# Products with the low halves of the weights, emitted two parts of the stream later

## The chip, the cores and the metric

The kernel runs on one core of one Trainium2 chip. The time is that of one execution on the device, in microseconds (us). Before the change it is 3813.72 us, the median of three runs (3813.32 to 3816.19).

## The reference

Two transformer blocks in float32 follow each other, for 256 tokens and 2048 features. The first mixes with an mLSTM and an S5 recurrence and has PEER (products with 16384 experts) in place of an FFN. The second is modulated by a vector `c` through `w_ada` and has three attention branches, gates and a SwiGLU FFN.

```python
z = rmsnorm(h, norm1_g) @ w_in                       # first block
...
h = h + jnp.concatenate([hm, ys], axis=-1) @ w_out
h = h + peer(rmsnorm(h, norm2_g), peer_wq, peer_subkeys, peer_u, peer_v)
...
mod = jax.nn.silu(c) @ w_ada + b_ada                 # second block: shifts, scales, gains
y = (g[:, :, 0] * (o_sb @ w_br_sb) + g[:, :, 1] * (o_dil @ w_br_dil) + g[:, :, 2] * (o_gla @ w_br_gla))
...
out = (jax.nn.silu(gate) * up) @ w_ffn_out
```

The weights are some 750 MB, and each is used once for all 256 tokens.

## The kernel before

All weights come in one stream. `raw` takes a chunk of 1024 columns on 128 partitions (512 KB) with a DMA on SyncE's queue (SP, L217) into one of four buffers named `raw`. `split` cuts a part of 512 columns from it: `wh`, the high half that one pass of TensorE (PE) keeps, is made by ScalarE (ACT, L226), and `wl = raw - wh` by VectorE (DVE, L227). Each has four buffers. With `x = xh + xl` split in the same way, a float32 product is the sum of three: `xl wh` (L253), `xh wh` (L254) and `xh wl` (L255), the last of which is called the low product here. `gemm` walks over column tiles, over chunks and parts of the inner dimension, and over the two halves of the tokens (`tb`), and so issues six matmuls for a part. When a column tile is complete it calls `cb(i, P)`, which takes the two sums `P` out of PSUM (name `g`, four banks).

PEER's weighted sum over the experts' rows, `peer_v`, does the same with a stream of its own: its weights `uev` are made per 128 experts on ACT and DVE (L1075), and the three products are L1087, L1088 and, low, L1089. Its sums fill all eight banks (`g` and `b`).

`ada` is a side job. It loads half rows of `w_ada` through the same `raw` buffers and SP queue, and multiplies each on DVE with silu(c), held as `xl` or `adac` (L889, with a sum into `macc`). A step of `peer_v` or `gemm` runs a bit of it: in `peer_v`, in the second `w_in` and in the gates one half row comes after each three chunks, here called a turn: three chunks are six parts.

Each engine works its instructions off in order. Which order that is, a scheduler decides as the program is built (`schedule_with_timeline_sim=True`), from the order in the code, the buffers and an estimate of its own.

Of the kernel before, what the change touches and what calls it, by code (L numbers as in the profile page):

```python
# [11 lines left out]
F32 = mybir.dt.float32  # L12
# [15 lines left out]
NEG = -1e30  # L28
RC = 1024
# [4 lines left out]
# gla gate, q, k, v | sb q, k | sb v | dil q, k | dil v | gla r  # L34
W2_TILES = [272, 256] + [512] * 3 + [512] * 3 + [512, 256] + [512] * 3 + [512, 256] + [512] * 2
FT = 44
LAST = [512] * 3 + [256] * 2            # less is left to do when the last tile ends
# half rows of w_ada that are done by the end of PEER's v, and by the start of the second block's FFN
ADA = 80, 160


def pack(w, widths):
    """column tiles of the widths, each in chunks of up to RC columns for each partition"""
    k = w.shape[0]
    out, o = [], 0
    for n in widths:
        z = w[:, o:o + n].reshape(k // 128, 128, n)
        for i in range(0, k // 128, RC // n):
            out.append(z[i:i + RC // n].transpose(1, 0, 2).ravel())
        o += n  # L50
    assert o == w.shape[1]
    return np.concatenate(out)
# [71 lines left out]

class Within:
    """tiles within a float32 tile [128, n]"""

    def __init__(self, ap):
        self.ap, self.off, self.bufs = ap, 0, {}
# [17 lines left out]
class Kern:  # L147
# [46 lines left out]
    def triangle(self, p):  # L194
        """free index minus partition index, where it isn't negative, and ones"""
# [11 lines left out]
    def stream(self, raws, sc, splits):  # L207
        """buffers of the weight stream: raw chunks of RC columns, parts of sc columns"""
# [11 lines left out]
    def split(self, r, n):  # L220
        """r = h + l, h with the bits that one pass of the tensor engine keeps"""
# [8 lines left out]
    def gemm(self, wname, widths, KT, xh, xl, cb, steps=1, base=0, ks=None):  # L230
        """out[t, n] = x[t, ks] W[ks, n], in column tiles; xh, xl: [128, ks, 256]; cb(i, [P0, P1])"""
# [3 lines left out]
        sc = self.stp[1]  # L235
        for i, wn in enumerate(widths):
# [3 lines left out]
            for k0 in range(ka, kb, per):  # L240
# [3 lines left out]
                for j0 in range(0, kn, sub):  # L244
                    jn = min(sub, kn - j0)
                    h, l = self.split(r[:, j0 * wn:(j0 + jn) * wn], jn * wn)
                    for j in range(jn):
                        k = k0 + j0 + j
                        hs, ls = h[:, j * wn:(j + 1) * wn], l[:, j * wn:(j + 1) * wn]
                        for tb in range(2):  # L250
# [4 lines left out]
                            nc.tensor.matmul(o, xh[:, k - ka, t], ls, start=False, stop=k == kb - 1)  # L255
                self.step(steps)
            cb(i, P)
            off += 128 * KT * wn
        return off

    def rstd(self, pool, ss, n, name="rstd", bufs=2):
        """(ss / n + eps) ** -0.5 for a tile of sums of squares"""
# [4 lines left out]
    def rsqrt(self, pool, v, name, bufs):  # L267
        """v ** -0.5: a guess from the bits, and Newton steps"""
# [11 lines left out]
    def transpose4(self, src_aps):  # L280
        """transposes up to four [128, 128] blocks into one bank"""
# [9 lines left out]
    def put_T(self, X, xh, xl, gain, q):  # L291
        """xh + xl = columns q of X[tb] [128, 2048], times gain, with features on partitions"""
# [9 lines left out]
    def norm_r(self, work, ss, name="rstd"):  # L302
        """1 / rms from ss: [128, 2, n] sums of squares of parts of the rows"""
# [4 lines left out]
    def norm_T(self, X, r, xh, xl, work, gain, shift, row=None):  # L308
        """xh + xl = X[tb] [128, 2048] times r[:, tb], row and gain, plus shift, with features on partitions"""
# [23 lines left out]
    # ------------------------------------------------------------------ first block  # L333
    def s5_params(self, p):
# [31 lines left out]
        pw = p.tile([128, 8, 2, 32], F32, name="s5pw")      # a^1 .. a^8  # L366
# [31 lines left out]
        # recurrence multipliers of a^8: [ar, ar], [-ai, ai]  # L398
# [3 lines left out]
        pn = p.tile([128, 8, 2, 32], F32, name="s5pn")      # imaginary parts of the powers, negated and not  # L402
# [4 lines left out]
        cn = prm[:, 96 + 1024:].rearrange("p (r m h) -> p r m h", r=2, m=32)    # c, minus its imaginary part  # L407
        cpad = p.tile([128, 2, 32, 32], F32, name="s5t0")   # the same, padded to 32 columns
# [8 lines left out]
        # taps -7 .. 7 of the convolution, of which the negative ones are zero  # L417
# [5 lines left out]
        self.Vt = self.xx.tile([128, 32, 2, 32], F32, name="X1")            # (hf, p), c, ri, m  # L423
        yield

    def s5_taps(self, p, q):
        """for the groups of quarter q: powers times B, and the taps K of the convolution within a chunk, to DRAM"""
# [3 lines left out]
        GB = self.GB[q] = p.tile([128, 2, 8, 8, 16], F32, name="s5q", bufs=2)      # (hf, p), ri, m, tau, h  # L431
# [16 lines left out]
        KS = self.pb.tile([128, 512], F32, name="e", bufs=2)          # (gr, o32), (hf, a), (tau, h)  # L448
# [14 lines left out]
        KT = self.pb.tile([128, 16, 16], F32, name="e", bufs=2)           # (tau, h), g, o  # L463
# [9 lines left out]
    def s5_put_u(self, p, uT):  # L473
        """uT: [(g8, h), (q, hf), 7 - j, c] to rows (7 - j, h), columns (g, c), for each quarter of the groups"""
# [3 lines left out]
        U = self.xx.tile([128, 64, 32], F32, name="X0")            # (7 - j, h), (q, hf, g8), c  # L478
# [8 lines left out]
    def s5_in(self, p, q):  # L487
        """V[g, c] = sum_j a^(7-j) B u on rows (gr, c), then on rows (hf, p)"""
# [4 lines left out]
        for a in range(2):  # L493
            gt = p.tile([128, 4, 2, 128], F32, name="s5x")     # (tau, h), gr, ri, (hf, p)
# [9 lines left out]
        VS = self.pb.tile([128, 2, 2, 128], F32, name="e", bufs=2)       # (gr, c), a, ri, (hf, p)  # L504
# [9 lines left out]
    def s5_states(self, p):  # L514
        """entering states of the 32 chunks of 8 tokens"""
# [14 lines left out]
    def s5_out(self, p, q, yg):  # L530
        """outputs of quarter q of the groups, on rows (i, o)"""
# [3 lines left out]
        t0 = p.tile([128, 8, 16, 16], F32, name="s5t0")         # (7 - j, h), i, g, o  # L535
# [4 lines left out]
        # C a^(i+1), real and minus imaginary parts  # L540
# [11 lines left out]
        YS = self.pb.tile([128, 512], F32, name="e", bufs=2)          # (gr, c), (hf, a), (i, o)  # L552
# [22 lines left out]
    def s5_glu(self, p, q, yg, ys):  # L575
        """yg: [(i, o), (q, hf, g8), c]; ys: [128, 8, 256] f32, features on partitions"""
# [1137 lines left out]
```

## Time and profile before

| | |
|---|---|
| median of three runs | 3813.72 us |
| span of the profiled execution | 3811.8 us |
| outside the span (median less span) | 1.9 us |
| PE busy | 3625.0 us, 95% |
| DVE busy | 2675.0 us, 70% |
| ACT busy | 1980.6 us, 52% |
| DMA | 766 MB, mean 201 GB/s |

The profile is of one execution. Its span goes from the first to the last instruction. The run from which it was taken has no separate time here, so the span stands beside the median. Busy shares are averages over stages with different limits; the stages are roughly: the first block until 590 us, PEER's scores and choice to 790, PEER's u to 1360, PEER's v to 2100, the second block's `w_in` and branches to 2573, the gates to 2937, `w_br` and `w_out` to 3090, and the FFN to the end.

### The profile page before, as it was taken

How to read it: one execution, taken by the hardware profiler on the slowest of the kernel's cores; microseconds unless marked ns; L12 is line 12 of the kernel's file. 1: busy time of each engine (PE TensorE's matmuls, PEld its weight loads, DVE VectorE, ACT ScalarE, POOL GpSimd, SP SyncE). 2: the span in 40 equal slices, each digit the busy share in tenths (PEclk: the TensorE clock that was granted, in tenths of full speed). 3: DMA queues.
4: the chain of work that ended last, by engine and by line, in shares of the span. 5: the costliest groups of instructions: out<-in, count | busy, mean ns of one | idle time of the engine just before them, and what ended most of it. 6: DMA issues, size and time to landing. Idle time of an engine off the chain costs nothing. (4 is left out here: it accounts for less than half of the span.)

```text
span 3811.8 us, 52802 instructions
## 1 busy us (share of the span) xinstructions
PE 3625.0 (95%) x17438; PEld 2954.6 (78%) x17438; DVE 2675.0 (70%) x5604; ACT 1980.6 (52%) x3487; POOL 457.9 (12%) x475
## 2 busy tenths in 40 slices
PE   8998998999999999999998899999998999999999
PEld 7776886888887877777766777887777888888888
DVE  7685789689999766666555878876656666665554
ACT  5555654555554454454444555764444455555443
POOL 1060003035555200000000011000000000000000
PEclk9998999999999999999999999999999999999999
DMA  7655654655555577776666665666666667776665
GB/s 206 183 158 153 194 171 150 187 172 172 173 169 163 174 244 233 232 234 230 220 223 215 216 216 175 204 212 226 225 230 228 201 197 236 236 236 198 184 200 164
DMA packets 228082, 766.07 MB, mean 201 GB/s; under 512 B 40480, under 2 KB 44448, under 8 KB 225376
## 3 DMA queue, kind: packets, MB, share of 16 engines
q1 hardware_dynamic: 225376, 748.57, 62.2%
q0 software_dynamic: 2432, 14.13, 1.0%
q8 instruction: 137, 2.24, 0.2%
q14 instruction: 137, 1.12, 0.1%
HBM read 753.23 MB, written 9.37 MB: 200 GB/s over the span
## 5 line engine op out<-in xcount | busy, mean ns | idle before, releaser
L226 ACT ACTIVATE wh<-raw 128x512 fp32r<-128x512 f32 (+2 forms) x2416 | 1490.7, 628 | 1588.6 <-PE g L254 710.5
L227 DVE TENSOR_TENSOR wl<-raw,wh 128x512 fp32r<-128x512 f32 (+2 forms) x2416 | 1653.6, 708 | 505.0 <-ACT wh L226 461.9
L253 PE MATMUL g<-wh,xl 128*128 128x512 f32 (+2 forms) x3296 | 1270.3, 386 | 9.6 <-ACT wh L226 9.0
L254 PE MATMUL g<-wh,xh 128*128 128x512 f32 (+2 forms) x3296 | 1264.9, 384 | 0.0
L255 PE MATMUL g<-wl,xh 128*128 128x512 f32 (+2 forms) x3296 | 1096.5, 388 | 53.6 <-DVE wl L227 53.0
L255 PEld LDWEIGHTS g<-wl,xh 128*128 128x128 f32 x3296 | 608.6, 189 | 191.2 <-DVE wl L227 83.7
L253 PEld LDWEIGHTS g<-wh,xl 128*128 128x128 f32 x3296 | 623.1, 189 | 131.1 <-ACT wh L226 12.6
L254 PEld LDWEIGHTS g<-wh,xh 128*128 128x128 f32 x3296 | 622.6, 189 | 116.3 <-issue 0.4
L889 DVE SCALAR_TENSOR_TENSOR raw<-raw,adac 128x1024 f32<-128x1024 f32 x112 | 141.9, 1267 | 252.3 <-DMA raw<-in_w_ada 252.3
L889 DVE SCALAR_TENSOR_TENSOR raw<-raw,xl 128x1024 f32<-128x1024 f32 x80 | 98.0, 1225 | 275.4 <-DMA raw<-in_w_ada 275.4
L1087 PE MATMUL g<-wh,uev 128*128 128x512 f32 x512 | 205.2, 401 | 1.3 <-DVE uev L1075 1.3
L1088 PE MATMUL g<-wh,uev 128*128 128x512 f32 x512 | 202.0, 395 | 0.0
L1087 PE MATMUL b<-wh,uev 128*128 128x512 f32 x512 | 200.1, 391 | 0.3 <-ACT wh L226 0.3
L1088 PE MATMUL b<-wh,uev 128*128 128x512 f32 x512 | 199.9, 390 | 0.0
L1089 PE MATMUL b<-wl,uev 128*128 128x512 f32 x512 | 148.3, 407 | 34.9 <-DVE wl L227 34.9
L1089 PE MATMUL g<-wl,uev 128*128 128x512 f32 x512 | 163.4, 399 | 18.8 <-DVE wl L227 18.7
L1032 POOL TENSOR_TENSOR e<-e,t 128x256 fp32r<-128x256 f32 x128 | 129.0, 1008 | 325.0 <-DVE e L1031 236.6
L253 PE MATMUL g<-wh,fl 128*128 128x512 f32 (+1 forms) x440 | 154.4, 351 | 0.0
L254 PE MATMUL g<-wh,fh 128*128 128x512 f32 (+1 forms) x440 | 154.2, 351 | 0.0
L1089 PEld LDWEIGHTS b<-wl,uev 128*128 128x128 f32 x512 | 90.4, 188 | 75.9 <-DVE wl L227 61.6
L1033 POOL TENSOR_TENSOR e<-e,t 128x256 fp32r<-128x256 f32 x128 | 137.1, 1071 | 9.9
L255 PE MATMUL g<-wl,fh 128*128 128x512 f32 (+1 forms) x440 | 132.7, 348 | 0.0
(529 smaller groups left out, 3539.8 us busy)
## 6 DMA issues: line engine op xcount, KB each, us to landing
raw<-in_peer_u SPq DMA_DIRECT2D x256, 512.0 KB, 3.6
raw<-in_peer_v SPq DMA_DIRECT2D x256, 512.0 KB, 4.7
raw<-in_w_in SPq DMA_DIRECT2D x192, 512.0 KB, 4.4
raw<-in_w_ada SPq DMA_DIRECT2D x192, 512.0 KB, 4.0
raw<-in_w_ffn_in SPq DMA_DIRECT2D x176, 512.0 KB, 4.1
raw<-in_w_gates SPq DMA_DIRECT2D x96, 512.0 KB, 4.2
raw<-in_w_ffn_out SPq DMA_DIRECT2D x88, 512.0 KB, 4.2
raw<-in_w_out SPq DMA_DIRECT2D x64, 512.0 KB, 4.2
```

The costliest lines, as they stand in the source:

```text
L226: nc.scalar.activation(h[:, :n], r, AF.Copy)
L227: nc.vector.tensor_tensor(l[:, :n], r, h[:, :n].bitcast(F32), op=OP.subtract)
L253: nc.tensor.matmul(o, xl[:, k - ka, t], hs, start=k == ka, stop=False)
L254: nc.tensor.matmul(o, xh[:, k - ka, t], hs, start=False, stop=False)
L255: nc.tensor.matmul(o, xh[:, k - ka, t], ls, start=False, stop=k == kb - 1)
L889: nc.vector.scalar_tensor_tensor(r, r, 1.0, cr[:, hf * RC:(hf + 1) * RC], op0=OP.mult, op1=OP.mult, accum_out=self.macc[:, j:j + 1])
L1032: E.tensor_tensor(o2[:, :, 1], f(o2[:, :, 0]), bc(f(self.wl), t), op=OP.mult)
L1033: E.tensor_tensor(o2[:, :, 0], f(o2[:, :, 0]), bc(f(self.wh), t), op=OP.mult)
L1087: nc.tensor.matmul(o, w[:, 1, t], h, start=i1 == 0, stop=False)
L1088: nc.tensor.matmul(o, w[:, 0, t], h, start=False, stop=False)
L1089: nc.tensor.matmul(o, w[:, 0, t], l, start=False, stop=i1 == 127)
```

## The change

`LAG = 2`. A class `Late` holds a list of jobs, each with the number of parts that it counts for. In `gemm` and in `peer_v` the two low products of a part go into the list; `late.run(LAG)` then emits the oldest until at most two are left. The call of `cb` goes into the list too, with zero parts, so it comes right behind its tile's last low products, while the next tile's high products are already emitted. Only at the end of the `gemm` or of `peer_v` is the list emptied. Buffers, counts of instructions and loads are left as they are. The docstrings and comments that the diff strips are not shown.

```diff
+LAG = 2
+class Late:
+    def __init__(self):
+        self.jobs, self.n = [], 0
+    def add(self, f, parts=1):
+        self.jobs.append((f, parts))
+        self.n += parts
+    def run(self, keep):
+        while self.jobs and (self.n > keep or not self.jobs[0][1]):
+            f, parts = self.jobs.pop(0)
+            self.n -= parts
+            f()
...
     def gemm(self, wname, widths, KT, xh, xl, cb, steps=1, base=0, ks=None):
+        late = Late()
         for i, wn in enumerate(widths):
...
                             nc.tensor.matmul(o, xl[:, k - ka, t], hs, start=k == ka, stop=False)
                             nc.tensor.matmul(o, xh[:, k - ka, t], hs, start=False, stop=False)
-                            nc.tensor.matmul(o, xh[:, k - ka, t], ls, start=False, stop=k == kb - 1)
+                        late.add(lambda P=P, k=k, ls=ls, wn=wn: [
+                            nc.tensor.matmul(P[tb][:, :wn], xh[:, k - ka, tb * 128:tb * 128 + 128], ls, start=False,
+                                             stop=k == kb - 1) for tb in range(2)])
+                        late.run(LAG)
                 self.step(steps)
-            cb(i, P)
+            late.add(lambda i=i, P=P: cb(i, P), 0)
             off += 128 * KT * wn
+        late.run(0)
...
     def peer_v(self, p, AT, half, steps=1):
-        ws = {}
+        ws, late = {}, Late()
...
-                nc.tensor.matmul(o, w[:, 0, t], l, start=False, stop=i1 == 127)
+            late.add(lambda: [nc.tensor.matmul(P[tb][n], w[:, 0, tb * 128:tb * 128 + 128], l, start=False,
+                                               stop=i1 == 127) for tb in range(2)])
+            late.run(LAG)
...
+        late.run(0)
         self.drain()
```

In the changed file `wl` is L245, the high products of `gemm` are L272 and L273 and its low ones L275, `uev` is L1098, and `ada`'s multiply is L912.

This is PE's list before, at the start of the first `gemm`: two parts.

```order
29 L253 MATMUL g<-wh,xl 128x512
30 L254 MATMUL g<-wh,xh 128x512
31 L253 MATMUL g<-wh,xl 128x512
32 L254 MATMUL g<-wh,xh 128x512
33 L255 MATMUL g<-wl,xh 128x512 x2
34 L253 MATMUL g<-wh,xl 128x512
35 L254 MATMUL g<-wh,xh 128x512
36 L253 MATMUL g<-wh,xl 128x512
37 L254 MATMUL g<-wh,xh 128x512
38 L255 MATMUL g<-wl,xh 128x512 x2
```

And this is PE's list after, at the same place. Rows 29 to 36 are the high products of the first two parts, and the piece begins with those of the third.

```order
37 L272 MATMUL g<-wh,xl 128x512
38 L273 MATMUL g<-wh,xh 128x512
39 L272 MATMUL g<-wh,xl 128x512
40 L273 MATMUL g<-wh,xh 128x512
41 L275 MATMUL g<-wl,xh 128x512 x2
42 L272 MATMUL g<-wh,xl 128x512
43 L273 MATMUL g<-wh,xh 128x512
44 L272 MATMUL g<-wh,xl 128x512
45 L273 MATMUL g<-wh,xh 128x512
46 L275 MATMUL g<-wl,xh 128x512 x2
```

The low products at row 41 are those of the first part; before they stood at row 33, ahead of the second part's high ones.

The scheduler also places other engines' instructions anew. This is DVE's list before, in the first half of `peer_v`, shortly ahead of the place where `half()` begins: two turns, with `uev` for each 128 experts.

```order
2282 L227 TENSOR_TENSOR wl<-raw,wh 128x512
2283 L889 SCALAR_TENSOR_TENSOR raw,macc<-raw,xl 128x1024
2284 L227 TENSOR_TENSOR wl<-raw,wh 128x512 x3
2285 L1075 TENSOR_TENSOR uev<-AT,uev 128x256
2286 L227 TENSOR_TENSOR wl<-raw,wh 128x512 x2
2287 L889 SCALAR_TENSOR_TENSOR raw,macc<-raw,xl 128x1024
2288 L227 TENSOR_TENSOR wl<-raw,wh 128x512 x2
2289 L1075 TENSOR_TENSOR uev<-AT,uev 128x256
2290 L227 TENSOR_TENSOR wl<-raw,wh 128x512 x4
2291 L1075 TENSOR_TENSOR uev<-AT,uev 128x256
2292 L227 TENSOR_TENSOR wl<-raw,wh 128x512
```

And this is DVE's list after, at about the same place.

```order
2278 L1098 TENSOR_TENSOR uev<-AT,uev 128x256
2279 L912 SCALAR_TENSOR_TENSOR raw,macc<-raw,xl 128x1024
2280 L245 TENSOR_TENSOR wl<-raw,wh 128x512 x4
2281 L1098 TENSOR_TENSOR uev<-AT,uev 128x256
2282 L245 TENSOR_TENSOR wl<-raw,wh 128x512 x2
2283 L912 SCALAR_TENSOR_TENSOR raw,macc<-raw,xl 128x1024
2284 L245 TENSOR_TENSOR wl<-raw,wh 128x512 x2
2285 L1098 TENSOR_TENSOR uev<-AT,uev 128x256
2286 L245 TENSOR_TENSOR wl<-raw,wh 128x512 x4
2287 L1098 TENSOR_TENSOR uev<-AT,uev 128x256
```

Before, one of two multiplies stands behind the first `wl` of a chunk, with three more `wl` behind it; after, it stands directly behind `uev`, with four. In the second half of `peer_v` the list of before has the order of the second piece too; the list of after has that order from the start of `peer_v`.

## Rows read from the trace of the kernel before

**Rows 1.** the page, part 1: busy us, share of span, instructions
```profile
PE 3625.0 (95%) x17438; PEld 2954.6 (78%) x17438; DVE 2675.0 (70%) x5604; ACT 1980.6 (52%) x3487; POOL 457.9 (12%) x475
```

**Rows 2.** four stretches: length, then busy time and instructions of each engine, TensorE's clock, DMA
```profile
590.00:680.00 90.00, 78.17 (x329) 59.17 (x328) 86.11 (x180) 41.59 (x63) 36.78 (x16) 0.98 0.50 150
1360.00:2100.00 740.00, 686.81 (x2882) 534.07 (x2881) 454.18 (x762) 362.65 (x601) 4.65 (x3) 0.99 0.68 228
2573.00:2937.00 364.00, 336.41 (x1432) 264.49 (x1431) 216.09 (x343) 164.22 (x272) 17.96 (x12) 1.00 0.68 226
3090.00:3811.00 721.00, 717.56 (x3442) 600.38 (x3440) 421.33 (x684) 352.72 (x601) 0.00 (x0) 1.00 0.66 210
```

**Rows 3.** what PE waited for, whole span: total us, times, longest us
```profile
PE g L255 <- DVE wl L227: 58.5, 62, 4.9
PE b L1089 <- DVE wl L227: 34.9, 33, 1.8
PE g L1089 <- DVE wl L227: 18.7, 17, 3.7
```

**Rows 4.** timeline of PE in the FFN: start us, us
```profile
3300.26 0.39 PE L253 MATMUL g<-wh,xl 128*128 128x512 f32 x1
...
3301.62 0.39 PE L253 MATMUL g<-wh,xl 128*128 128x512 f32 x1
```

**Rows 5.** what DVE waited for in PEER's v, 1360 to 2100 us
```profile
DVE raw L889 <- DMA raw<-in_w_ada: 271.7, 78, 4.8
DVE wl L227 <- PE g L1089: 6.2, 6, 1.4
```

**Rows 6.** timeline of DVE early in PEER's v; in brackets the wait before
```profile
1562.78 1.22 DVE L889 SCALAR_TENSOR_TENSOR raw<-raw,xl 128x1024 f32<-128x1024 f32 x1 [3.71 <-DMA raw<-in_w_ada]
...
1572.55 1.23 DVE L889 SCALAR_TENSOR_TENSOR raw<-raw,xl 128x1024 f32<-128x1024 f32 x1 [3.27 <-DMA raw<-in_w_ada]
```

**Rows 7.** timeline of SP's queue in the same stretch
```profile
1557.38 0.33 SPq L217 DMA_DIRECT2D raw<-in_w_ada  x1
...
1566.97 0.33 SPq L217 DMA_DIRECT2D raw<-in_w_ada  x1
...
1575.62 0.33 SPq L217 DMA_DIRECT2D raw<-in_w_ada  x1
```

**Rows 8.** what PE waited for in the gates, 2573 to 2937 us
```profile
PE g L255 <- DVE wl L227: 25.8, 30, 1.8
```

**Rows 9.** what DVE waited for in the gates
```profile
DVE raw L889 <- DMA raw<-in_w_ada: 141.2, 39, 5.3
```

**Rows 10.** what PE waited for from 590 to 680 us
```profile
PE g L255 <- DVE wl L227: 11.8, 15, 2.5
```

**Rows 11.** the page, part 5, weight loads: busy us, mean ns, idle before
```profile
L255 PEld LDWEIGHTS g<-wl,xh 128*128 128x128 f32 x3296 | 608.6, 189 | 191.2 <-DVE wl L227 83.7
...
L254 PEld LDWEIGHTS g<-wh,xh 128*128 128x128 f32 x3296 | 622.6, 189 | 116.3 <-issue 0.4
```

**Rows 12.** timeline of DVE late in PEER's v
```profile
1910.21 1.23 DVE L889 SCALAR_TENSOR_TENSOR raw<-raw,xl 128x1024 f32<-128x1024 f32 x1 [4.59 <-DMA raw<-in_w_ada]
...
1919.41 1.23 DVE L889 SCALAR_TENSOR_TENSOR raw<-raw,xl 128x1024 f32<-128x1024 f32 x1 [3.84 <-DMA raw<-in_w_ada]
```

**Rows 13.** timeline of SP's queue in the same stretch
```profile
1903.91 0.33 SPq L217 DMA_DIRECT2D raw<-in_w_ada  x1
...
1913.88 0.33 SPq L217 DMA_DIRECT2D raw<-in_w_ada  x1
...
1923.60 0.33 SPq L217 DMA_DIRECT2D raw<-in_w_ada  x1
```

**Rows 14.** L889 alone in two stretches of PEER's v, early and late
```profile
1378.00:1712.00 334.00, 45.63 (x74) 0.99 0.70 234
1741.00:2095.00 354.00, 45.63 (x74) 1.00 0.66 220
```

**Rows 15.** what ScalarE waited for from 0 to 100 us
```profile
ACT wh L226 <- DMA raw<-in_w_in: 13.1, 2, 11.6
```

## The prediction, made blind

> **What bounds the kernel now.** The busy table of the page first: TensorE (PE) is busy for 95% of the span, the next engine, VectorE (DVE), for 70% [rows 1]. So a gain has to come from gaps of PE, and a loss is a new gap. The table by stretch shows where the gaps lie: the second block's FFN has next to none, PEER's v (1360 to 2100 us) loses 740 - 687 = 53 us, the gates (2573 to 2937) 28, the stretch from 590 to 680 loses 12 [rows 2]. The list of what PE waited for names the low products in front: L255 for 58.5 us in 62 waits, and L1089, which is PEER's v alone, for 34.9 + 18.7 = 53.6 us in 50 [rows 3]. These 112 us are what the change can reach at the very most, since it gives `wl`, the low half that DVE makes, two more parts of time before PE asks for it. A part (512 columns) is six matmuls, and at full speed 1.36 us of PE: 3301.62 - 3300.26, so 0.227 us a matmul [rows 4].
>
> Next, why `wl` is late at each place. If DVE is only behind by a bit, two parts cure it; if DVE has less throughput than PE there, PE meets the same rate two parts later, and nothing is won. The three big places are of the second kind.
>
> In PEER's v DVE itself waits: 271.7 us in 78 waits at L889, each for a half row of w_ada that SP issued and that hasn't landed [rows 5]. The timeline shows the loop. SP issues a w_ada load at 1557.38; the multiply L889 starts as it lands, 1562.78; the next w_ada issue is at 1566.97, the next multiply at 1572.55, the next issue at 1575.62 [rows 6, 7]. From issue to multiply are 5.4 and 5.6 us, from multiply to the next issue 4.2 and 3.1: two turns take 18.2 us, thus 9.1 us for six parts on which PE has 6 x 1.36 = 8.2 us of work. The turn holds: the load, the multiply, the `wl` instructions behind it on DVE (which works in order), the release of the raw buffers, SP's issues behind them. No product of PE stands in it: DVE waited for L1089 to give back a `wl` buffer for 6.2 us in six waits only [rows 5]. PE idles in each turn because a turn is longer than its work, so asking later for `wl` doesn't shorten it. The gates look alike: 25.8 of the 58.5 us at L255 [rows 8], beside 39 waits of DVE for w_ada, 141.2 us [rows 9]. From 590 to 680 DVE is busy for 86.1 of 90 us [rows 2], and the 11.8 us at L255 there [rows 10] are its rate.
>
> **The change part by part.** 1. *Products.* None is added or removed. At 6 x 0.227 us a part PE's work is the same: 0. I looked for a shared weight load that the split could tear apart, since L254 and L255 both hold `xh`: each of the two lines has 3296 loads of its own for 3296 products, 189 ns each, beside the matmuls [rows 11]. Hence 0. The Trainium skill ("TensorE: Matmul & The Clock Gate", "Step-by-step: what each phase is for") says that a loaded operand can serve many matmuls; by that, two products with one `xh` emitted together would cost one load, and the change would undo the saving. The counts say that this kernel never took it.
>
> 2. *Isolated waits.* What is left of L255 outside the gates and outside 590 to 680 is 58.5 - 25.8 - 11.8 = 20.9 us in 62 - 30 - 15 = 17 waits, 1.2 us each. Here lateness is passing, and the change can help. How much: a full ring of four `wl` has three parts ready behind the one that PE reads, 3 x 1.36 = 4.1 us, with and without the lag, so cover grows only where the ring wasn't full, by two parts of high products, 2 x 4 x 0.227 = 1.8 us a wait. Bounds: 0 and -20.9. I take -8, below the middle, since the ring caps both.
>
> 3. *The order on DVE in PEER's v.* The scheduler places `wl`, `uev` and L889 anew, because their readers moved. Before, up to about 1720 us, every second multiply stands one `wl` later ("`wl`, multiply, `wl` x3"), and from there to the end the multiply comes straight after `uev` ("`uev`, multiply, `wl` x4"). The changed kernel's list has the second pattern from the start. Its price is in the trace of before, which has both. For two turns, multiply to next issue: early 4.2 + 3.1 = 7.3 us, late 3.7 + 4.2 = 7.9 [rows 6, 7, 12, 13], since one more `wl` stands between the multiply and the release. That is 0.6 us for a pair, and with 18.5 pairs early 11 us. Over whole stretches: 37 multiplies (74 records with the accumulator reads) took 334 us early and 354 late [rows 14]: 20 us. I take the middle, +15.5; bounds +11 and +20. 0 belongs to a rival.
>
> 4. *Buffers are held longer.* A `wl` buffer comes free two parts later against the high products, 2.7 us, and so, where PE sets the pace, does the raw buffer behind it, and the load into that. Where loads are covered this costs nothing: four raw buffers are eight parts, 10.9 us, for a load that takes 5.4 us even in the loop. It shows where a load is late anyway: ScalarE once waited 11.6 us for a w_in chunk [rows 15]. One such place at 2.7 us: +2.7; bounds 0 and twice that.
>
> 5. *Ends.* At the end of a `gemm` and of PEER's v the last two parts of low products stand alone, and the callback comes behind them, with at most 4 x 0.227 x 2 = 1.8 us. Within a `gemm` the next tile's products cover that. Where a stage ends and its successor waits for the last column, PE still does the same work; I put +1.8 for PEER's v, whose result is normalised at once, and 0 for the rest.
>
> Sum: -8 + 15.5 + 2.7 + 1.8 = +12. On the profiled span, 3811.8, that gives 3823.8. The median of the runs shown, 3813.7, is 1.9 us above it, so **3825.7**. Late next, where a `wl` wait goes, is the high product: L253 and L1087 wait for `wh`, which comes from the same raw chunks.
>
> **The rivals.** *No change (A).* The 20 us between the early and the late half aren't due to DVE's order but to slower transfers; 220 against 234 GB/s could be read so [rows 14], though a longer turn for the same bytes gives that too. Then term 3 is gone: 3813.7 - 3.5 = 3810.2. For it: the late half's longer issue-to-multiply times, 6.3 and 5.5 us [rows 12, 13]. Against: the 0.6 us of a pair stand between multiply and issue, where DVE waits for no transfer.
>
> *Faster (B).* The same, and the 17 isolated waits all go, because the ring is seldom full there: 3813.7 - 20.9 + 1.8 = 3794.6. It decides when term 3 is under 12 us and the cover works in most places. In its extreme the waits of PEER's v and the gates are passing too, and 100 us go; the 9.1 us turns speak against it.
>
> *Slower by the ring (C).* With `wl` held two parts longer, DVE waits inside the loop for PE to return one. The six waits of before are 1.0 us each [rows 5]. If a third of the 74 turns gets one, 25 us come on top of the forecast: 3851. Against: in the loop PE is the starved side, so buffers lie free. The Trainium skill ("Perfetto Trace Analysis", "Optimization Strategy") reads a gap that repeats for a stretch as a sign of too few buffers; by that, holding each longer makes the repeated gap wider, which is C.
>
> *Weight loads (D).* If loads had been shared, 3296 + 1024 more at 189 ns would be up to 816 us. The counts exclude it almost wholly.
>
> **How the numbers follow.** Within 0.2%, 7.6 us, a measurement of this kernel can't tell from no change: same is 3806.1 to 3821.3. The forecast's case has 0.57, and its own range is 3814 to 3836 (term 3 at 11 or 20, term 2 at -13 or 0, term 4 at 0 or 5.4); 0.07 of it lies within the bound, 0.50 above. A has 0.15, all within. B has 0.22, faster, C 0.05 and D 0.01, slower. So faster 0.22, same 0.22, slower 0.56. The range reaches down to just above B's price, 3797, and up to just below C's, 3848. What no row prices is how the scheduler's new order falls out between 100 and 430 us and between 2100 and 2573, where chains of small operations share DVE with `wl`; the width holds some 15 us of that either way.
>
> **What would show it.** Right: in PEER's v the first 37 multiplies take about 350 us instead of 334, PE's gap there grows, the waits for `wl` persist under the new line of the low products, and 590 to 680 and the gates keep their time. Wrong in term 2: the waits at low products outside these places are gone with their time, or stay. Wrong in term 3: the early half keeps 334 us with the new order (A). The forecast fails most plainly if PEER's v gets shorter (B's extreme) or if DVE waits for low products there (C).

## The result and the profile after

The changed kernel was slower: 3836.8 us (median of four runs) against 3815.0, a ratio of 1.0055 (95% interval 1.0037 to 1.0073). Run again beside other kernels, the same file gave 3822.3 against 3813.6, 1.0024 (1.0014 to 1.0033). So the loss is +9 to +22 us; the forecast was +12, on the right side. 3836.8 lies within 3797 to 3848 and just above the 3814 to 3836 of the forecast's own case. The changed kernel's two profiled executions have spans of 3827.4 and 3813.0 us against 3811.8.

PE does the same work: busy for 3625.0 us before [rows 1] and 3625.1 after. The table by stretch has the four that were shown of before [rows 2], moved to where the same loads stand:

```profile
592.00:682.00 90.00, 78.56 (x324) 61.04 (x323) 88.35 (x176) 39.72 (x62) 34.30 (x16) 0.94 0.47 145
1363.00:2107.00 744.00, 685.45 (x2872) 529.92 (x2872) 451.79 (x760) 358.64 (x599) 4.65 (x3) 1.00 0.69 226
2597.00:2954.00 357.00, 333.62 (x1417) 262.29 (x1416) 211.07 (x334) 151.97 (x261) 17.89 (x12) 0.99 0.71 229
3107.00:3827.00 720.00, 715.98 (x3435) 599.50 (x3434) 420.44 (x684) 340.57 (x599) 0.00 (x0) 1.00 0.68 211
```

PEER's v lost a little (PE's gap there is 58.6 us, 53.2 before, and 47.7 in e8, the changed kernel's second profile), the gates gained, the FFN and the stretch in which DVE is full stayed. What PE waited for, whole span, answers to [rows 3]:

```profile
PE g L275 <- DVE wl L245: 50.2, 52, 4.2
PE b L1112 <- DVE wl L245: 38.1, 36, 2.8
PE g L1112 <- DVE wl L245: 21.2, 30, 2.2
PE g L272 <- ACT wh L244: 16.5, 12, 4.5
```

The low products wait for 109.5 us in all, against 112.1 before: two parts more of time took almost nothing away (in e8 it is 99.3). The high products of `gemm` wait for `wh` for 16.5 us (10.0 in e8); before it was

```profile
PE g L253 <- ACT wh L226: 9.3, 4, 7.8
```

Where the time went is best seen between events that both programs have. This table is worked out from SP's timeline: each border is the issue of the first (or 129th, or last) chunk of a weight, from the span's start. Columns: to the first chunk of PEER's v; to its 129th; to its 256th; on to the first chunk of the gates (the second block's `w_in` and branches); to the first of w_ffn_in; to the end.

```
kernel, profiled execution  to v    v 1-128  v 129-256   w_in    gates   to end
before                     1326.5    386.8    400.3     429.7    501.4    767.2
changed                    1329.5    403.2    388.2     446.7    492.8    767.0
e8 changed, again          1326.6    395.5    381.8     448.9    492.3    767.8
e1 lag 0                   1341.3    390.7    400.7     436.0    494.0    767.7
e2 lag in PEER's v only    1334.2    392.0    400.1     440.1    491.5    768.1
e3 lag in gemm only        1337.7    400.8    391.1     448.2    496.8    767.8
e4 lag 1                   1344.3    409.8    403.9     446.3    491.9    768.1
e5 lag 2, halves apart     1333.0    396.1    386.7     445.2    486.6    767.4
e6 own buffer, before      1328.6    389.5    361.4     429.8    502.4    767.2
e7 own buffer, changed     1331.9    390.7    358.0     447.2    494.0    767.7
e9 no lag in w_in          1336.4    397.7    392.9     436.9    493.6    768.6
e10 two wl buffers         1413.4    399.7    393.3     473.3    515.6    832.4
e11 e6, lag in the gates   1325.8    392.5    360.3     432.4    489.4    767.4
e12 before, lag in gates   1327.3    392.2    409.6     434.4    492.2    767.0
```

In the first profile of the changed kernel the sum is +3.0 + 16.4 - 12.1 + 17.0 - 8.6 - 0.2 = +15.5, within rounding the 15.6 us by which its span is longer. In the second (e8) it is +0.1 + 8.7 - 18.5 + 19.2 - 9.1 + 0.6 = +1.0, for 1.2. Two losses and two gains stand behind the forecast's +12, and those of PEER's v don't keep their sum: its 256 chunks took 4 us longer than before in one execution and 10 us less in the other.

A border is the issue of a load, and PE may have done more or less of its work by then. The stretches of `w_in` before and after, then those of the gates before and after:

```profile
2113.60:2543.30 429.70, 404.20 (x2066) 338.96 (x2065) 350.12 (x839) 262.47 (x501) 32.54 (x20) 0.98 0.62 204
2120.90:2567.60 446.70, 412.34 (x2085) 342.78 (x2084) 348.67 (x843) 264.76 (x507) 33.15 (x20) 0.98 0.61 197
2543.30:3044.60 501.30, 465.15 (x2037) 371.53 (x2036) 305.27 (x496) 234.92 (x398) 26.11 (x20) 0.98 0.67 221
2567.60:3060.40 492.80, 459.70 (x2022) 366.78 (x2021) 303.12 (x492) 222.91 (x393) 26.04 (x20) 0.99 0.70 224
```

After, 19 more of PE's matmuls fall into `w_in` and 15 fewer into the gates; at 0.227 us that is some 4 and 3 us of work that only crossed a border. With PE's own work as the border (the start of the first high product of each `gemm`), `w_in` takes 409.5 us before and 420.4 and 422.6 in the two profiles of the changed kernel, and gates, `w_br` and `w_out` together 514.6, 510.6 and 510.9: +11 and +13, and -4.

**The early half of PEER's v.** DVE's and SP's timeline of the changed kernel, at the place of [rows 6, 7]:

```profile
1556.99 1.23 DVE L912 SCALAR_TENSOR_TENSOR raw<-raw,xl 128x1024 f32<-128x1024 f32 x1 [4.39 <-DMA raw<-in_w_ada]
...
1566.50 1.23 DVE L912 SCALAR_TENSOR_TENSOR raw<-raw,xl 128x1024 f32<-128x1024 f32 x1 [3.59 <-DMA raw<-in_w_ada]
...
1567.65 2.49 DVE L245 TENSOR_TENSOR wl<-raw,wh 128x512 fp32r<-128x512 f32 x4
```

```profile
1561.18 0.33 SPq L235 DMA_DIRECT2D raw<-in_w_ada  x1
...
1570.17 0.33 SPq L235 DMA_DIRECT2D raw<-in_w_ada  x1
```

From multiply to next issue are now 1561.18 - 1556.99 = 4.19 and 1570.17 - 1566.50 = 3.67 us, as in the late half of before [rows 12, 13], and not 4.19 and 3.07. The same 37 multiplies, early and late, answer to [rows 14]:

```profile
1381.50:1730.90 349.40, 45.65 (x74) 1.00 0.68 222
1759.40:2103.50 344.10, 45.63 (x74) 1.00 0.68 227
```

Early 349 instead of 334, as forecast; late 344 instead of 354, which wasn't. Late, multiply to next issue is 3.94 us on the mean of 37 turns in both; issue to multiply is 5.34 us and not 5.62, so the w_ada loads themselves took less time.

**The second block's w_in.** Waits of ACT, then of SP, in this stretch (2118 to 2543 us before, 2125 to 2567 after). Before:

```profile
ACT wh L226 <- PE g L254: 52.3, 66, 4.0
ACT wh L226 <- DMA raw<-in_w_in: 27.0, 18, 3.2
ACT wh L226 <- DVE wl L227: 10.9, 9, 4.4
```

```profile
SPq L217 <- DVE wl L227: 172.6, 78, 15.2
```

After:

```profile
ACT wh L244 <- DMA raw<-in_w_in: 37.8, 27, 4.5
ACT wh L244 <- DVE wl L245: 37.0, 24, 4.5
ACT wh L244 <- PE g L273: 18.9, 17, 5.3
```

```profile
SPq L235 <- DVE wl L245: 222.1, 102, 15.7
```

Before, ACT mostly waits for PE to give a `wh` buffer back: it is ahead. After, it waits for chunks, and SP waits 50 us more for `wl` to release a raw buffer. PE meets that as late `wh`, after against before:

```profile
PE g L272 <- ACT wh L244: 7.2, 8, 2.0
```

```profile
PE g L253 <- ACT wh L226: 0.2, 1, 0.2
```

### The profile page after: what moved, and what is told of

It reads as the page before. It is cut to its first block, busy times and chain, and to the rows that moved or that the text cites. A ratio compares the mean times of both kernels' runs of the same rounds, so it can differ in the third digit from the quotient of the medians.

```text
span 3827.4 us, 52877 instructions
## 1 busy us (share of the span) xinstructions
PE 3625.1 (95%) x17438; PEld 2950.3 (77%) x17438; DVE 2679.3 (70%) x5604; ACT 1953.4 (51%) x3487; POOL 447.8 (12%) x475
## 5 line engine op out<-in xcount | busy, mean ns | idle before, releaser
L244 ACT ACTIVATE wh<-raw 128x512 fp32r<-128x512 f32 (+2 forms) x2416 | 1469.7, 627 | 1645.3 <-PE g L273 620.2
L245 DVE TENSOR_TENSOR wl<-raw,wh 128x512 fp32r<-128x512 f32 (+2 forms) x2416 | 1647.5, 708 | 457.3 <-PE g L275 385.2
L272 PE MATMUL g<-wh,xl 128*128 128x512 f32 (+2 forms) x3296 | 1269.6, 387 | 18.3 <-ACT wh L244 16.5
L273 PE MATMUL g<-wh,xh 128*128 128x512 f32 (+2 forms) x3296 | 1260.4, 384 | 0.0
L275 PE MATMUL g<-wl,xh 128*128 128x512 f32 (+2 forms) x3296 | 1009.8, 388 | 49.0 <-DVE wl L245 48.4
L275 PEld LDWEIGHTS g<-wl,xh 128*128 128x128 f32 x3296 | 604.7, 189 | 186.0 <-DVE wl L245 73.6
L272 PEld LDWEIGHTS g<-wh,xl 128*128 128x128 f32 x3296 | 623.7, 189 | 145.2 <-ACT wh L244 24.8
L273 PEld LDWEIGHTS g<-wh,xh 128*128 128x128 f32 x3296 | 623.8, 189 | 116.7 <-issue 0.4
L912 DVE SCALAR_TENSOR_TENSOR raw<-raw,adac 128x1024 f32<-128x1024 f32 x112 | 140.4, 1253 | 250.0 <-DMA raw<-in_w_ada 250.0
L912 DVE SCALAR_TENSOR_TENSOR raw<-raw,xl 128x1024 f32<-128x1024 f32 x80 | 98.0, 1225 | 289.4 <-DMA raw<-in_w_ada 289.4
L1112 PE MATMUL g<-wl,uev 128*128 128x512 f32 x512 | 162.7, 400 | 21.5 <-DVE wl L245 21.2
L1055 POOL TENSOR_TENSOR e<-e,t 128x256 fp32r<-128x256 f32 x128 | 118.7, 929 | 332.7 <-DVE e L1054 180.0
L272 PE MATMUL g<-wh,fl 128*128 128x512 f32 (+1 forms) x440 | 150.0, 349 | 0.0
L273 PE MATMUL g<-wh,fh 128*128 128x512 f32 (+1 forms) x440 | 150.0, 350 | 0.0
L1056 POOL TENSOR_TENSOR e<-e,t 128x256 fp32r<-128x256 f32 x128 | 138.5, 1085 | 8.3
L1112 PEld LDWEIGHTS g<-wl,uev 128*128 128x128 f32 x512 | 93.7, 189 | 54.3 <-DVE wl L245 36.7
```

What stands on the lines that cost most here:

```text
L244: nc.scalar.activation(h[:, :n], r, AF.Copy)
L245: nc.vector.tensor_tensor(l[:, :n], r, h[:, :n].bitcast(F32), op=OP.subtract)
L272: nc.tensor.matmul(o, xl[:, k - ka, t], hs, start=k == ka, stop=False)
L273: nc.tensor.matmul(o, xh[:, k - ka, t], hs, start=False, stop=False)
L275: nc.tensor.matmul(P[tb][:, :wn], xh[:, k - ka, tb * 128:tb * 128 + 128], ls, start=False, stop=k == kb - 1) for tb in range(2)])
L912: nc.vector.scalar_tensor_tensor(r, r, 1.0, cr[:, hf * RC:(hf + 1) * RC], op0=OP.mult, op1=OP.mult, accum_out=self.macc[:, j:j + 1])
```

## Experiments

Ratios are to runs of the kernel before on the same chip in the same session, with the 95% interval. Kernels of one session: e1 to e4; e5 to e8; e9 to e12. Each session had another chip.

**e1, lag 0**, a control.

```diff
-LAG = 2
+LAG = 0
```

> The changed code with a lag of 0: the low products of a part come right behind its high ones again. In PEER's v DVE's list has the order of the kernel before (19 turns with the multiply behind one wl in the early half). Theory 1 (the time went where DVE's order in the loop on w_ada got longer, plus what the lag does in the second block's w_in): as the kernel before, 3815 us within 6. Rival (the lists and the callback behind the low products cost by themselves): slower by more than 8 us.

3831.7 us, 1.0040 (1.0025 to 1.0055). It wasn't like the kernel before: by the totals a lag of 0 costs as much as one of 2 (1.0055 and 1.0024), so they don't show what the two parts cost. Its lists differ from those of before: the code now puts the low products of both token halves behind both high pairs, as PE's list has it for nearly all of the 1996 parts of `gemm`, where the scheduler had placed some 1310 so before; and the callback comes later. In its profile PEER's v took as long as before within 5 us; +15 us had come ahead of it, some 9 of them in PEER's u. That is a `gemm` too; e2, with the same order there, lost 3 us in it, so most of the 9 may be this execution's. The second `w_in` is 6 us longer, the gates 7 shorter.

**e2 and e3, the lag in one place only.** In e2 `gemm` has no lag, in e3 `peer_v` has none:

```diff
-                        late.run(LAG)
+                        late.run(0)
```

```diff
-            late.run(LAG)
+            late.run(0)
```

> Lag of 2 in PEER's v alone, 0 in every gemm. DVE's list in PEER's v keeps the order of the kernel before, though its low products are late. Theory 1: the early 37 multiplies take 334 us as before, not 350, and the whole is 3812 to 3820 us. Rival 2 (holding wl two parts longer in PEER's v stretches the loop): the early 37 multiplies take about 350 us and the whole is near 3828. Rival 3 (lateness after all): PEER's v gets shorter by 10 us or more.

> Lag of 2 in every gemm, 0 in PEER's v, whose products are in the order of the kernel before. DVE's list in PEER's v nevertheless has the longer order (multiply straight behind uev, four wl behind it) from the start. Theory 1: the early 37 multiplies take about 350 us though no low product there is late, and the second block's w_in loses 10 to 15 us as in the changed kernel; whole 3828 to 3838 us. Rival 2: the early 37 take 334 us; the whole is below 3822.

e2: 3833.1 us, 1.0049 (1.0034 to 1.0063). e3: 3842.1, 1.0065 (1.0051 to 1.0079). The early 37 multiplies of e2, and those of e3:

```profile
1387.70:1725.80 338.10, 45.64 (x74) 0.99 0.70 232
```

```profile
1391.00:1737.10 346.10, 45.64 (x74) 1.00 0.68 225
```

Late low products with the old order on DVE took 338; low products in time with the longer order, 346. One program's executions differ by as much there (e8), so the pair alone doesn't settle it. What does is multiply to next issue, mean of the early 37 turns: 3.62 to 3.64 us in the four profiles with the old order (before, e1, e2, e12), 3.93 in the six with the longer one (changed, e8, e3, e4, e5, e9), 0.30 us a turn or 11 us in all. Not the lag in PEER's v but DVE's list, which the scheduler carries there from the stages ahead, has this price. Both totals lie above what was expected, by some 13 and 4 us. PEER's v as a whole is 5 us longer than before in either profile; e2 lost more in the second `w_in` (+10), with a lag of 0 there and a lower granted clock, 0.96 against 0.98 before, and ahead of PEER's v (+8).

**e4, lag 1** (`LAG = 1`).

> A lag of 1 part everywhere. DVE's list in PEER's v has the longer order from the start. Theory 1: the early 37 multiplies take about 350 us as with lag 2, since the price hangs on the order and not on the length of the lag; whole 3825 to 3838 us. Rival 2 (the price grows with the time that a wl buffer is held): half of the loss, about 3824 us, and 342 us early.

3855.2 us, 1.0100 (1.0085 to 1.0115): more than the changed kernel in either of its sessions, so the loss doesn't grow with the length of the lag. The early 37 took 359 us, of which the order explains 11; the rest is loads that took longer in this execution. The total is above what either theory gave.

**e5, lag 2 with the token halves apart**: each low product is a job of its own, so that a lag of 0 would be PE's list of before, row for row.

```diff
-                        late.add(lambda P=P, k=k, ls=ls, wn=wn: [
-                            nc.tensor.matmul(P[tb][:, :wn], xh[:, k - ka, tb * 128:tb * 128 + 128], ls, start=False,
-                                             stop=k == kb - 1) for tb in range(2)])
-                        late.run(LAG)
+                            late.add(lambda P=P, k=k, ls=ls, wn=wn, tb=tb:
+                                nc.tensor.matmul(P[tb][:, :wn], xh[:, k - ka, tb * 128:tb * 128 + 128], ls, start=False,
+                                                 stop=k == kb - 1))
+                            late.run(2 * LAG)
```

> Lag of 2 parts, but each token half's low product is emitted by itself, behind that half's high pair, as in the kernel before; with a lag of 0 this is the list of the kernel before to the row. Theory 1 (the lag costs: the longer order on DVE in PEER's v, and late high products in the second block's w_in): near the changed kernel, 3828 to 3842 us. Rival 4 (what costs is that the low products of both halves were put together behind both high pairs, which lag 0 did too): within 6 us of the kernel before.

3819.7 us, 1.0025 (1.0013 to 1.0037): like the changed kernel in the same session (1.0024), and 6 us above the kernel before, short of theory 1's range and at the edge of rival 4's. Beside a lag, putting the halves together in the code makes no difference that the totals show. Its stretches move as the changed kernel's do: early v +9, late v -14, `w_in` +16, gates -15.

**e6 and e7, a buffer of its own for w_ada** in PEER's v, in the kernel before and in the changed one.

```diff
-    def ada(self, cr, j0, j1, every=1):
+    def ada(self, cr, j0, j1, every=1, own=None):
...
-            r = self.raw(w[nb * 128:(nb + 1) * 128, hf * RC:(hf + 1) * RC], RC)
+            src = w[nb * 128:(nb + 1) * 128, hf * RC:(hf + 1) * RC]
+            if own is None:
+                r = self.raw(src, RC)
+            else:
+                r = own[:, :RC]
+                nc.sync.dma_start(r, src)
...
-            self.add_side(self.ada(self.act.tile([128, D], F32, name="xl"), 0, ADA[0], 3), 1)
+            cw = self.act.tile([128, 2, D], F32, name="xl")
+            self.add_side(self.ada(cw[:, 0], 0, ADA[0], 3, cw[:, 1]), 1)
```

> The kernel before, with a raw buffer of its own for the w_ada half rows in PEER's v (in the unused half of the tile that holds silu(c) there), so that their loads leave the ring of four. Theory 1 (the waits at the low products of PEER's v come from the turn load, multiply, wl, release, next load): the waits at L1089 fall from 53.6 us below 15 us, and the time by 35 to 50 us, to 3765 to 3780 us. Rival 3 (the low products are late for DVE's work, whatever DVE waits for): the waits stay above 35 us and the time above 3800.

> The changed kernel with the same buffer of its own. Theory 1: without the turn DVE's order in PEER's v has no price, so the changed kernel loses less against its counterpart than the 0.55% of the pair without it: PEER's v as long as in e6 within 5 us, and the rest of the loss (10 to 17 us in the second block's w_in and branches) stays; 3775 to 3795 us. Rival 2: PEER's v is longer than in e6 by 10 us or more.

e6: 3771.3 us, 0.9894 (0.9877 to 0.9911). e7: 3794.7, 0.9952 (0.9939 to 0.9965). What PE waited for in PEER's v in e6, where the low products are L1094:

```profile
PE g L1092 <- DVE uev L1080: 21.8, 27, 3.6
PE b L1094 <- DVE wl L227: 3.0, 1, 3.0
...
PE g L1094 <- DVE wl L227: 2.1, 4, 0.9
```

From 53.6 us at low products to 5.1, with `wl` asked for as early as ever. PE waits for `uev` instead, but only for 21.8 us, and PEER's v is 36 us shorter. The turn through the shared ring was the cause, and the lag couldn't remove it. (e6 gives both a fifth buffer and a ring that `w_ada` doesn't share; five shared buffers weren't tried.) The Trainium skill ("Perfetto Trace Analysis", "Optimization Strategy") reads a gap that repeats for a stretch as a possible lack of buffers; this trace agrees, with raw chunks as what was lacking. (The multiplies also gather in the first half there, where the chunks for PEER's v and w_ada together moved 263 GB/s; only the second half got shorter, by 39 us.) In e7 PEER's v is as long as in e6 within 3 us, and `w_in` keeps its +17: the price on DVE's order is gone with the turn, and the other loss isn't. The totals don't follow: e7 is 23 us above e6 (0.6%), where less than 0.55% was expected and the changed kernel of the same session (e8) is only 9 us above the kernel before. So they don't show a loss that goes with the turn.

**e8, the changed kernel again.**

> The changed kernel once more, for a second profile. In the first, the late half of PEER's v was 12 us shorter than before though no list of an engine differs in pattern there, since the w_ada loads took 5.35 us from issue to multiply and not 5.58. If that hangs on the execution, this profile has another time there (by 5 us or more) and the early half keeps 3.94 us from multiply to next issue; if it hangs on the change, the late half is again 10 to 14 us shorter.

3822.3 us, 1.0024. Multiply to next issue is as in the first profile; the early 37 took 341 us, the late 338:

```profile
1378.40:1719.80 341.40, 45.64 (x74) 1.00 0.67 227
1748.60:2086.70 338.10, 45.65 (x74) 1.00 0.68 229
```

The same program differs by 8 and 6 us between two executions in these halves. That the late half is shorter than before came again, and by more than the 10 to 14 us of the expectation.

**e9, no lag in the second `w_in`** (the argument of `late.run` in `gemm` is 0 there, LAG elsewhere).

> The changed kernel, with a lag of 0 in the second block's w_in alone. In five profiles with a lag there, the stretch from the last PEER v load to the first gates load took 15 to 19 us longer than before, with high products waiting for wh. Theory 1 (the lag there costs it): the stretch takes 432 to 440 us, and not 444 to 447 as with the lag; the whole 8 to 15 us less than the changed kernel, 3808 to 3820 us on this scale. Rival 4 (any other order of these lists costs as much): the stretch stays at 444 or more.

3825.2 us, 1.0019 (1.0006 to 1.0031). The stretch took 436.9 us, in the range for theory 1, and SP's waits are back at the size of before: it waited 158.5 us for `wl` and not 222.

```profile
SPq L235 <- DVE wl L245: 158.5, 81, 15.1
```

The total did not follow: its profiled execution had 10 us more ahead of PEER's v, and the ratio can't be told from 1.0024. The lag's loss in `w_in` is shown by the stretch, not by the total: 432.4 to 440.1 us in the five profiles of the new code with a lag of 0 there (e1, e2, e9, e11, e12), 445.2 to 448.9 in the six with a lag of 1 or 2. Before, it was 429.7, so 3 to 10 of the 17 us come without a lag there.

**e10, two `wl` buffers in the kernel before.**

```diff
-        l = self.st.tile([128, sc], F32R, name="wl", bufs=bufs)
+        l = self.st.tile([128, sc], F32R, name="wl", bufs=2)
```

> The kernel before, its products in their old order, with two wl buffers in place of four: the lag of two holds two more of four. Theory 1 (a lag costs because wl, and with it the raw chunk, is held for longer): the stretch of the second block's w_in grows by 10 us or more over the kernel before, with more waits of the high products for wh, and the whole by 15 to 60 us. Rival (the loss there is only in how the lists fall): the stretch stays within 6 us of the kernel before.

4029.6 us, 1.0560 (1.0540 to 1.0580), far over the 15 to 60 us of theory 1. `w_in` grew by 44 us, but not as theory 1 said. In that stretch (2220 to 2680 us here) PE waited for

```profile
PE g L255 <- DVE wl L227: 38.7, 34, 5.1
...
PE g L253 <- ACT wh L226: 0.8, 1, 0.8
```

that is for low products, not for `wh`. What DVE waited for there, and behind it the same of the changed kernel (2125 to 2567 us):

```profile
DVE wl L227 <- PE g L255: 26.1, 47, 1.2
```

```profile
DVE wl L245 <- PE g L275: 3.5, 6, 1.2
```

With two buffers DVE stands waiting for PE to return one; with the lag it doesn't. So a short ring isn't what the lag did in `w_in`: there `wl` is made later although its buffers are free.

**e11 and e12, a lag in the gates alone**, halves apart as in e5 (not shown again), a lag of 0 elsewhere; e11 with e6's buffer, e12 without.

```diff
-    def gemm(self, wname, widths, KT, xh, xl, cb, steps=1, base=0, ks=None):
+    def gemm(self, wname, widths, KT, xh, xl, cb, steps=1, base=0, ks=None, lag=0):
...
-                    self.gemm("w_gates", [512] * 3, KD, xh, xl, cb_g, base=n * 3 * D * 512)
+                    self.gemm("w_gates", [512] * 3, KD, xh, xl, cb_g, base=n * 3 * D * 512, lag=LAG)
```

> The kernel with a w_ada buffer of its own in PEER's v (e6), and a lag of 2, halves apart, in the gates alone, the one stage that was shorter in all profiles with a lag. Theory 1 (a lag helps where the low products' waits are passing and hurts nowhere else if it is left out there): 5 to 12 us less than e6, 3760 to 3768 us. Rival 5 (the gates gained because the stages before them ran late, or by chance): within 4 us of e6.

> The kernel before with a lag of 2, halves apart, in the gates alone. Theory 1: the gates' stretch (first gates load to first w_ffn_in load, 501 us before) takes 488 to 495 us, and the whole 3802 to 3808 us. Rival 5: the stretch stays at 499 us or more and the whole within 4 us of the kernel before.

e11: 3769.5 us, 0.9885 (0.9867 to 0.9903). e12: 3810.9, 0.9985 (0.9975 to 0.9996). The gates' stretch took 489 and 492 us, not 502 and 501. e12's total is 6 us under that of before, less than theory 1 had; e11's is only 2 us under e6's, which was of another session, so the totals of this pair leave rival 5 standing. e11 is the fastest version found, by 47 us against the kernel before, nearly all of it through the buffer.

## Why the prediction was right

**1. Products: right.** PE's busy time is the same.

**2. Isolated waits: too hopeful.** Forecast -8. From 592 to 682 us L275 waited 11.2 us, in the gates (2597 to 2954) 17.8; that leaves 50.2 - 11.2 - 17.8 = 21.2 us elsewhere, against 20.9 before. Nothing was saved. (In e8 it is 52.1 - 11.0 - 18.5 = 22.6.)

**3. DVE's order in PEER's v: right for the early half, not for the stage.** Multiply to next issue grew as worked out, 0.6 us a pair. Over the four profiles with the short order, that of before, the first 128 chunks took 386.8 to 392.2 us, mean 390.4 (before, e1, e2, e12); over the six with the long order 395.5 to 409.8, mean 400.5 (changed, e8, e3, e4, e5, e9): 10 us, the lower bound of 11 and not the 15.5 taken. (e10, with another ring, and the three with a buffer of their own are left out.) Rival A, that the order costs nothing, falls with that, but it had half of the 20 us right: of the kernel before, multiply to issue differs by 0.31 us between early and late turns, issue to multiply, the loads, by 0.27. And the stage as a whole paid nothing on the mean: all 256 chunks took 787 to 802 us with the short order, mean 793, and 777 to 814 with the long one, mean 791. In e8 they took less than before, which the prediction had named as its plainest failure.

**4. Buffers held longer: mis-sized, and by another way.** Forecast +2.7, bounds 0 and 5.4. It is +15 to +19 us in the five profiles with a lag of 2 in the second `w_in` (changed, e8, e3, e5, e7), and +17 at lag 1; bordered by PE's own work it is +10 to +13.5 in all six. I had argued that four raw buffers cover a load; there they don't, since DVE has the branches' work too and makes `wl` late enough that SP waits for the release. That the high product would be late next came true at this place. But `wl` isn't late because PE holds its buffers: DVE waited for that for 3.5 us. Nor does more work stand ahead of it: DVE is busy for 350.1 us in this stretch before and for 348.7 after. What grew is DVE's wait for results of ACT inside the branches' work. Before and after, three of its places:

```profile
DVE w L1405 <- ACT w L1404: 1.1, 1, 1.1
DVE dlse L1358 <- ACT dlse L1357: 0.8, 1, 0.8
DVE oG L1491 <- ACT T L1588: 0.2, 1, 0.2
```

```profile
DVE w L1431 <- ACT w L1430: 2.9, 2, 2.2
DVE dlse L1384 <- ACT dlse L1383: 2.5, 1, 2.5
DVE oG L1517 <- ACT T L1614: 2.3, 1, 2.3
```

All such waits (those for `wh` left out) come to 9.2 us before and 20.9 after. They are 18.0 to 21.5 us in the six profiles with a lag in this `gemm`, and 6.2 to 9.4 in the seven others with four `wl` buffers. So the lists of DVE and ACT meet less well there with a lag; which move of the scheduler does it wasn't tried.

**5. Ends.** Too small to be seen.

**What the forecast missed.** The gates were to stay, as a turn like PEER's v. They gained 9 us in both profiles (4 bordered by PE's own work), and 9 in e12, where the lag is there alone. The step that failed is "the gates look alike". In PEER's v DVE waited next to nothing for `wh` before; in the stretch of the gates (2543 to 3045 us) it did, and ACT, which makes `wh`, waited for PE to return a buffer. Before, DVE's row and ACT's:

```profile
DVE wl L227 <- ACT wh L226: 34.5, 47, 3.1
```

```profile
ACT wh L226 <- PE g L254: 139.3, 169, 5.9
```

The changed kernel (2568 to 3060 us), again DVE and ACT:

```profile
DVE wl L245 <- PE g L275: 30.8, 46, 1.5
...
DVE wl L245 <- ACT wh L244: 4.9, 6, 2.1
```

```profile
ACT wh L244 <- PE g L273: 77.7, 62, 8.8
```

So PE did stand in the gates' turn, by way of the `wh` buffers. With a lag the high products, the only readers of `wh` beside DVE's `wl`, run ahead, and the buffers come back sooner: ACT's wait for them falls by 62 us, and to 57.5 in e12. DVE then stands at the end of its own ring instead. But the gain doesn't need this: with a lag of 0 in the gates they are 7 us shorter in e1 and 10 in e2, and ACT waits as long as before. In e1 (2569 to 3063 us):

```profile
ACT wh L244 <- PE g L273: 149.8, 178, 4.9
```

PE's list there is nearly that of before, too: both low products of a part stand behind both high pairs in 245 parts of 256, and in 230 before. What shortens the gates thus stays open. The changed kernel, e1, e2 and e12 share, against before, a later place of the callback; that was not tried by itself.

The late half of PEER's v was the second miss: 7 to 19 us less than before in all profiles with a lag of 2 in most of `gemm` (changed, e8, e3, e5, e9), but not with lag 1 or 0. DVE's order is the same, and the loads' time differs; what shortens them stays open.

So in the first profile the forecast's total came from some +16 early in PEER's v (11 of them DVE's order) where +15.5 was forecast, +17 where +2.7 was, 0 where -8 was, and gains of about 9 and 12 us that weren't forecast at all; 3 us came ahead of PEER's v. That these add up to nearly +12 is luck: in both profiles only `w_in` and the gates together, +8 and +10, kept their size, and the forecast had next to nothing there. The sign came from the one, the number from misses that cancel. (The range of the forecast's own case was mis-added as well: its bounds, 20, 0, 5.4 and 1.8 on 3813.7, reach to 3841 and not to 3836.) Rival B's extreme, lateness in PEER's v, falls with e6. C, DVE held at a ring by PE in the loop, didn't come there: DVE waited there for low products for 2.1 us in all (before, 7.5: the 6.2 of the prediction leave out 1.3 on the banks `b`). Nor did D.

## What to carry to other kernels

Giving a consumer more time can help only where its producer is late in passing; here no such gain was seen. Where the producer itself waits in a turn (load, work, release, next load), look for the buffer that closes the turn: one buffer of its own gave 1.1%, two parts of lag nothing. A scheduler that places all engines anew can charge for an edit at a place that the edit doesn't touch, so compare each engine's list there, and read the price from a stretch of the old trace that happens to have the new order, engine's part and load's part apart. And a sum that comes out right isn't yet a mechanism that is right: check each term, in more than one profile. A lag frees one ring and fills another: ask which buffers, far up the stream, are now released later.

## What the runs showed of the hardware

A load of 512 KB took a different time in different executions of one program, with issues at the same distances: in PEER's v the 37 early w_ada turns of the changed kernel took 349 and 341 us, the late ones 344 and 338, though DVE's part of a turn, multiply to next issue, was the same in both (3.93 us on the mean, early). Issue to multiply was 5.53 and 5.33 us on the mean of the early turns; with 37 turns to a half, 0.2 us a load is 7 us. So a single profile couldn't tell a stage's change of less than some 8 us. The ratio of the changed kernel moved by 0.3% between two sessions, while the medians of the kernel before stayed within 0.1% (3813.6 to 3817.0 us); why is open.
